# A hybrid decoder layer on one core: the first output gates' weight tile is cast later, and the filling of the attention stage starts from an account of -500

## The chip, the cores and the metric

The kernel runs on one core of one Trainium2 chip, as one launch. The metric is the device time of that core in microseconds. The engines are TensorE (PE in the profile, its weight loads PEld), VectorE (DVE), ScalarE (ACT), GpSimd (POOL) and SyncE (SP), which issues most of the DMAs.

## The reference, cut to what matters

One decoder layer on 1024 tokens and 16 meta tokens, width 1024: half a SwiGLU, a mixer of two parallel head groups, half a SwiGLU again. The change lies in the mixer:

```python
u = rms_norm(h, mix_norm) @ w_in
hq, hf, hi, hg, sq, sk, sv = split(u)
# stick-breaking attention, 8 heads of 64, in blocks of 128 queries
z = q @ k.T * scale
log_beta, log_keep = log_sigmoid(z), log_sigmoid(-z)      # masked to earlier keys
w = exp(log_beta + suffix_sum(log_keep))                  # product of (1 - sigmoid) behind
out = w @ v
# HGRN2, 4 heads: queries, forget gates, values and output gates
f = lb + (1 - lb) * sigmoid(hf);  k = (1 - lb) * sigmoid(-hf)
q = silu(hq);  gate = silu(hg)
```

All of it is float32. The kernel reaches that precision by splitting each operand into a rounded half and the rest, and by three products for each: high by high, low by high, high by low.

## The kernel before, in words

**Stages.** First the first SwiGLU, then the mixer's input projection, the attention (the braid), the HGRN2 heads with the output projection, and the second SwiGLU. TensorE runs in the order in which the program was written there (a manual schedule for that engine alone). The other engines' order is made at compile time by a list scheduler from dependences and the order of writing, and an engine works through its queue in order. `issue_after(x)` sets that what is written inside it stands behind `x`, on `x`'s engine.

**The weights.** `split_w` (L215) loads a 128-column tile of `w_in` into a float32 tile `raw` (L227, a DMA in SyncE's queue, 512 KB; two buffers), lets ScalarE cast it to the high part (L232) and VectorE subtract that for the low part (L234). `col_tile` (L237) is its form for a column.

**The braid** (L1719) runs the attention. A job is a pair of query blocks of one head; the eight heads have four jobs each, with 144 and 272, 912 and 1040, 400 and 528, 656 and 784 keys. In a job there are score pieces (`sb_scores`, L1646): two matmuls into one of two banks `z` (L1665, L1666), two sigmoids on ScalarE (`keep` L1667, `sig` L1668), a running product on VectorE (a scan, L1671, which needs the constant tile `begin`, L2209, in the bank of an earlier projection) and a multiplication on GpSimd (L1678). Two rounds later come its flips: transposes of `sig` into one of two banks (L1515, L1571), split by ScalarE (L1643) and VectorE (L1644). Three rounds later come the products with the values (L1592, L1594). Round n so holds the scores of job n, the flips of job n - 2 and the values of job n - 3.

**The filling.** Between these pieces the braid lays steps of the HGRN2 projections (`hgrn_fill`, L1131), 76 at most. A step is 12 matmuls (L249 to L251), half of a piece of 512 (queries, output gates) or 256 to 272 columns (values, forget gates). The columns go head by head, as values, forget gates, queries, output gates. The first head's values and forget gates are projected ahead of the braid, so the braid's first step belongs to its queries. `part` (L1172) does a step; the first step of each column also takes the next column's tile, so the braid's first step loads and splits the tile of the first output gates. Behind the second half of a piece `use` (L1140) evacuates it: for forget gates two sigmoids on ScalarE (L1154, L1155) into staging tiles `st` (four buffers), two scalings on VectorE (L1156, L1159) and two stores (L1160, L1164); for queries and gates a sigmoid (L1162) and a multiplication (L1163). In the braid the filling has one bank.

**The account.** Every round adds to `owed` 1.22 times the written cost of its own pieces (0.84 for each score column, 107 for each flip, 240 for each value step). While `owed` is above 0 a step is taken and its cost, 12 (0.42 n + 13), is subtracted. The steps of a round are spread evenly over it:

```python
            owed += share * sum(t for _, t, _ in now)
            more = []
            while owed > 0:
                step = next(fill, None)
                if step is None:
                    break
                more.append(step)
                owed -= step[0]
            now += [(at + (i + 0.5) / len(more), t, f) for i, (t, f) in enumerate(more)]
```

Of the kernel before, what the change touches and what calls it, by code (L numbers as in the profile page):

```python
# [15 lines left out]
AF = mybir.ActivationFunctionType  # L16
# [4 lines left out]
P = 128  # L21
# [28 lines left out]
class Block:  # L50
# [161 lines left out]
            (dst[3], lambda r: kept(3, sub, r[0], r[1])),  # L212
        ]

    def split_w(self, view, parts=None):  # L215
        nc = self.nc
        n = int(np.prod(view.shape[1:]))
        if parts is not None:
            got = []
            for i, tag in enumerate(self.w_tags):  # L220
                t = self.wp.tile([P, n], F32R, tag=tag, name="w" + "hl"[i], bufs=self.w_bufs)
                self.last_load = nc.sync.dma_start(t.bitcast(F32), parts[:, i])
                got.append(t)
            return got
        raw = self.wp.tile([P, n], F32, tag="raw", name="raw", bufs=self.raw_bufs)
        to = raw.rearrange("p (k f) -> p k f", k=view.shape[1]) if len(view.shape) == 3 else raw
        self.last_load = nc.sync.dma_start(to, view)  # L227
        hi = self.wp.tile([P, n], F32R, tag="wh", name="wh", bufs=self.w_bufs)
        if self.split_on_vector:
            nc.vector.tensor_copy(hi, raw)  # L230
        else:
            self.rounded = nc.scalar.copy(hi, raw)  # L232
        lo = self.wp.tile([P, n], F32R, tag="wl", name="wl", bufs=self.w_bufs)
        nc.vector.tensor_sub(lo, raw, hi.bitcast(F32))  # L234
        return hi, lo

    def col_tile(self, w, col):  # L237
        return self.split_w(
            w[:, col : col + P].rearrange("(k p) f -> p k f", p=P), self.parted.get(col)
        )  # L240

    def product(self, ps, w, xh, xl, c0, n, ks=None):
# [888 lines left out]
    def hgrn_fill(self, xh, xl, pool, dst):  # L1131

        nc = self.nc
        plan, cols = self.heads_plan, self.columns_of_heads()
        self.stores, self.level_banks = [], "zo"

        def staged(n):
            return pool.tile([P, 512], F32, tag="st", name="st", bufs=4)[:, :n]

        def use(kind, h, ps, c0, n):  # L1140
            s = slice(c0, c0 + n) if kind in "vf" else slice(c0 - META, c0 - META + n)
            t = staged(n)
            if c0 >= HALVES[1][0] and kind != "g":
                ps = ps[:, ::-1]
                at = s.start + HALVES[1][0] + T - 2 * c0 - n
                s = slice(at, at + n)
            if kind == "v":
                nc.scalar.copy(t, ps)
                with self.tc.issue_after(self.last_load.ins):
                    nc.sync.dma_start(dst[kind][h, :, s], t)  # L1150
                return
            elif kind == "f":
                k = staged(n)
                nc.scalar.activation(t, ps, AF.Sigmoid)  # L1154
                nc.scalar.activation(k, ps, AF.Sigmoid, scale=-1.0)  # L1155
                nc.vector.tensor_scalar(  # L1156
                    t, t, self.lbc[:, h : h + 1], self.lb[:, h : h + 1], ALU.mult, ALU.add
                )
                nc.vector.tensor_scalar_mul(k, k, self.lbc[:, h : h + 1])  # L1159
                nc.sync.dma_start(dst["k"][h, :, s], k)  # L1160
            else:
                nc.scalar.activation(t, ps, AF.Sigmoid)  # L1162
                nc.vector.tensor_mul(t, t, ps)  # L1163
            store = lambda: nc.sync.dma_start(dst[kind][h, :, s], t)  # L1164
            if (kind, h) == plan[-1] and c0 == HALVES[1][0]:
                self.stores.append(store)
            else:
                store()

        kept = {}  # L1170

        def part(i, ci, c0, n, half):  # L1172
            if ci == 0 and half == 0:
                kept["w"] = self.ahead_w.pop(cols[i])
                for c in cols[i + 1 : i + (3 if i == 0 else 2)]:
                    if c not in self.ahead_w:
                        self.ahead_w[c] = self.col_tile(self.a["w_in"][0], c)
                kept["round"] = self.rounds[cols[1]]
            if half == 0:
                kept["ps"] = self.proj_bank(n)  # L1180
            self.product(
                kept["ps"], kept["w"], xh, xl, c0, n, range(4 * half, 4 * half + 4)
            )
            if half == 1:
                with self.tc.issue_after(kept["round"]) if i == 0 else ExitStack():
                    use(*plan[i], kept["ps"], c0, n)

        for i, (kind, _) in enumerate(plan):
            for ci, (c0, n) in enumerate(PIECES if kind in "vf" else HALVES):
                for half in range(2):  # L1190
                    yield 12 * (n * 0.42 + 13), lambda a=(i, ci, c0, n, half): part(*a)
# [454 lines left out]
    def sb_scores(self, pool, qs, ks, b, sigs):  # L1646
        nc = self.nc
        nk = META + P * (b + 1)
        pieces = -(-nk // 512)
        size = -(-nk // pieces)  # L1650
        size += size % 2
        q = qs[:, b * P : (b + 1) * P]
        kept = []

        def piece(s0, n):
            last = s0 + n == nk
            if last:
                keep = pool.tile([P, nk + 1], F32, tag="keep", name="keep", bufs=3)
                sig = pool.tile([P, nk], F32, tag="sig", name="sig", bufs=6)
                nc.gpsimd.memset(keep[:, nk : nk + 1], 1.0)  # L1660
                kept.append(keep)
                sigs.append(sig)
            keep, sig = kept[0], sigs[-1]
            z = self.pz.tile([P, n], F32, tag="z", name="z")
            nc.tensor.matmul(z, q, ks[0][:, s0 : s0 + n], start=True, stop=False)  # L1665
            nc.tensor.matmul(z, q, ks[1][:, s0 : s0 + n], start=False, stop=True)  # L1666
            nc.scalar.activation(keep[:, s0 : s0 + n], z, AF.Sigmoid, scale=-1.0)  # L1667
            nc.scalar.activation(sig[:, s0 : s0 + n], z, AF.Sigmoid)  # L1668
            first, end = max(s0, 1), nk + 1 if last else s0 + n
            kv = keep[:, first:end][:, ::-1]  # L1670
            nc.vector.tensor_tensor_scan(  # L1671
                out=kv, data0=kv, data1=self.begin[:, : end - first] if last
                else self.begin[:, :1].broadcast_to([P, end - first]),
                initial=0.0 if last else keep[:, end : end + 1],
                op0=ALU.mult, op1=ALU.max if last else ALU.bypass,
            )
            if s0 == 0:
                nc.gpsimd.tensor_mul(sig, sig, keep[:, 1 : nk + 1])  # L1678

        return [  # L1680
            (n * 0.84, lambda s0=s0, n=n: piece(s0, n))
            for s0 in reversed(range(0, nk, size)) for n in [min(size, nk - s0)]
        ]
# [35 lines left out]
    def braid(self, jobs, fill, share, turn, value):  # L1719


        waiting = []
        owed = 0.0
        at = 0
        while True:
            job = next(jobs, None)
            for lag, steps in zip((0.0, turn, value), job or ()):
                spans = [1.0 if lag == turn else t for t, _ in steps]
                done = 0.0
                for span, (t, f) in zip(spans, steps):  # L1730
                    waiting.append((at + lag + (done + span / 2) / sum(spans), t, f))
                    done += span
            if not waiting:
                break
            now = [x for x in waiting if x[0] < at + 1]
            waiting = [x for x in waiting if x[0] >= at + 1]
# [9 lines that stand above are left out]
            for _, _, f in sorted(now, key=lambda x: x[0]):  # L1746
                f()
            at += 1
# [672 lines left out]
```

## Time and profile before

| | |
|---|---|
| median of 3 runs | 1938.81 us (1938.69 to 1940.38) |
| the profiled execution | 1938.33 us |
| its span, first to last instruction | 1936.6 us |
| TensorE, matmuls busy | 1915.8 us (99%) |
| VectorE busy | 1394.2 us (72%) |
| ScalarE busy | 847.4 us (44%) |
| GpSimd busy | 451.4 us (23%) |
| granted TensorE clock | 1.000 |

Durations in a row are those of one profiled execution. Matmuls are pipelined: a row of 0.39 us can be followed by the next 0.23 us later, and the distance between starts is the price of one. In the rows in order of time the columns are the start in us from the span's start, the length in us, the engine, the line, the operation, what it writes and reads, its shape and how many were merged; brackets give the idle time of that engine before it and what ended it. `proj` is a bank of a projection, `z` one of scores, `flip` one of transposes, `oacc` one of values.

### The profile page before, as it was taken

How to read it: one execution, taken by the hardware profiler on the slowest of the kernel's cores; microseconds unless marked ns; L12 is line 12 of the kernel's file. 1: busy time of each engine (PE TensorE's matmuls, PEld its weight loads, DVE VectorE, ACT ScalarE, POOL GpSimd, SP SyncE). 2: the span in 40 equal slices, each digit the busy share in tenths (PEclk: the TensorE clock that was granted, in tenths of full speed). 3: DMA queues.
4: the chain of work that ended last, by engine and by line, in shares of the span. 5: the costliest groups of instructions: out<-in, count | busy, mean ns of one | idle time of the engine just before them, and what ended most of it. 6: DMA issues, size and time to landing. Idle time of an engine off the chain costs nothing.

```text
span 1936.6 us, 30253 instructions
## 1 busy us (share of the span) xinstructions
PE 1915.8 (99%) x10637; PEld 1620.7 (84%) x10637; DVE 1394.2 (72%) x2184; ACT 847.4 (44%) x1712; POOL 451.4 (23%) x625
## 2 busy tenths in 40 slices
PE   9999999999999999999999999999999999999999
PEld 7888888888888888889998988888888888888887
DVE  7977778877678665567777776667577767766774
ACT  7523343334444545356666635433223332344443
POOL 3010100101000003133333342210545544530000
PEclk9999999999999999999999999999999999999999
DMA  7266788757975416765454178646544444479473
GB/s 220 89 175 169 244 280 257 232 199 272 382 238 183 138 42 154 188 182 150 135 155 123 57 267 246 154 185 211 170 128 133 135 127 134 128 251 315 147 233 114
DMA packets 381687, 355.54 MB, mean 184 GB/s; under 512 B 129040, under 2 KB 284560, under 8 KB 381536
## 3 DMA queue, kind: packets, MB, share of 16 engines
q1 hardware_dynamic: 360768, 288.98, 49.3%
q0 software_dynamic: 20768, 64.63, 9.6%
q8 instruction: 84, 1.38, 0.3%
q14 instruction: 67, 0.55, 0.1%
HBM read 237.95 MB, written 115.57 MB: 183 GB/s over the span
## 4 chain that ended last, share of the span: by engine, by line
PE 92%; DVE 3%; DMA 2%; ACT 1%; issue 1%; SPq 0%; POOL 0%; DVEq 0%; POOLq 0%; ACTq 0%
PE o L735 22%; PE qb L452 18%; PE qc L452 12%; PE qa L452 12%; PE proj L249 5%; PE proj L251 5%; PE proj L250 5%; PE flip L1515 2%; PE wo L250 1%; PE wo L251 1%; PE wo L249 1%; PE mq L1014 1%; PE oacc L1594 1%; PE oacc L1592 1%; PE z L1665 1%
## 5 line engine op out<-in xcount | busy, mean ns | idle before, releaser
L452 PE MATMUL qb<-T,wh 128*128 128x512 f32 x1056 | 343.7, 390 | 1.4 <-DVE u L484 1.4
L452 PEld LDWEIGHTS qb<-T,wh 128*128 128x128 f32 x1056 | 198.2, 188 | 45.8 <-issue 3.5
L452 PE MATMUL qa<-B,wh 128*128 128x512 f32 x696 | 227.6, 392 | 0.3 <-ACT B L838 0.2
L362 DVE TENSOR_TENSOR wl<-s,wh 128x512 fp32r<-128x512 f32 x160 | 165.8, 1036 | 69.1 <-ACT wh L360 68.2
L249 PE MATMUL proj<-xh,wh 128*128 128x512 f32 (+2 forms) x640 | 212.7, 332 | 1.1 <-ACT kT L1391 0.6
L735 PE MATMUL o<-t,w 128*128 128x512 f32 x924 | 212.1, 390 | 0.0
L251 PE MATMUL proj<-xl,wh 128*128 128x512 f32 (+2 forms) x640 | 209.3, 327 | 0.7 <-DVE xl L1984 0.7
L735 PE MATMUL o<-parts 128*128 128x512 f32 x924 | 209.6, 389 | 0.0
L250 PE MATMUL proj<-xh,wl 128*128 128x512 f32 (+2 forms) x640 | 208.9, 326 | 0.0
L452 PE MATMUL qb<-T,wl 128*128 128x512 f32 x528 | 205.6, 389 | 0.0
L735 PEld LDWEIGHTS o<-t,w 128*128 128x128 f32 x924 | 172.8, 188 | 37.1 <-issue 0.8
L735 PEld LDWEIGHTS o<-parts 128*128 128x128 f32 x924 | 173.5, 188 | 36.0
L360 ACT CAST wh<-s 128x512 fp32r<-128x512 f32 x160 | 99.5, 622 | 186.6 <-PE qb L452 141.6
L452 PEld LDWEIGHTS qa<-B,wh 128*128 128x128 f32 x696 | 130.5, 188 | 29.2 <-issue 1.0
L360 ACT CAST wh<-raw 128x512 fp32r<-128x512 f32 x120 | 74.4, 621 | 143.2 <-PE qc L452 101.3
L452 PE MATMUL qa<-B,wl 128*128 128x512 f32 x348 | 135.5, 389 | 0.0
L249 PEld LDWEIGHTS proj<-xh,wh 128*128 128x128 f32 x640 | 120.9, 189 | 12.7 <-ACT st L1155 1.2
L251 PEld LDWEIGHTS proj<-xl,wh 128*128 128x128 f32 x640 | 120.9, 189 | 11.8 <-DVE xl L1984 1.2
L250 PEld LDWEIGHTS proj<-xh,wl 128*128 128x128 f32 x640 | 121.1, 189 | 9.2
L452 PEld LDWEIGHTS qb<-T,wl 128*128 128x128 f32 x528 | 99.1, 188 | 20.3
L452 PE MATMUL qc<-T,wh 128*128 128x512 f32 x352 | 115.9, 391 | 0.0
L452 PE MATMUL qc<-B,wh 128*128 128x512 f32 x352 | 114.6, 389 | 0.0
(400 smaller groups left out, 3832.5 us busy)
## 6 DMA issues: line engine op xcount, KB each, us to landing
raw<-in_ffn_w_in_dram SPq DMA_DIRECT2D x176, 256.0 KB, 3.9
raw<-in_ffn_w_out_dram SPq DMA_DIRECT2D x112, 256.0 KB, 4.5
w2in<-both SPq DMA_DIRECT2D x28, 512.0 KB, 4.0
raw<-in_w_in_dram SPq DMA_DIRECT2D x25, 512.0 KB, 4.3
ks<-kD SPq DMA_DIRECT2D x32, 260.0 KB, 4.8
wout<-both SPq DMA_DIRECT2D x16, 512.0 KB, 3.9
wh<-w2in SPq DMA_DIRECT2D x27, 256.0 KB, 3.1
wl<-w2in SPq DMA_DIRECT2D x27, 256.0 KB, 3.3
```

What stands on the lines that cost most here:

```text
L249: nc.tensor.matmul(ps, wh[:, s], xs, start=k == 0, stop=False)
L250: nc.tensor.matmul(ps, wl[:, s], xs, start=False, stop=False)
L251: nc.tensor.matmul(ps, wh[:, s], xl[:, k, c0 : c0 + n], start=False, stop=k == nk - 1)
L360: nc.scalar.copy(hi, src)
L362: self.block_lo = nc.vector.tensor_sub(lo, src, hi.bitcast(F32))
L452: nc.tensor.matmul(ps, a[:, k, :], b[:, k, :], start=start and k == 0 and i == 0, stop=k == 3 and i == 2, skip_group_check=True,)
L735: nc.tensor.matmul(banks[bank][m], y[:, m * P : (m + 1) * P], z, start=start and at == 0 and e == 0, stop=q == nq - 1 and e == 2, skip_gro ...
L1014: nc.tensor.matmul(ps[at : at + 32, :], self.xm[:, 4 * h + k, :], got[i, h][:, k, :], start=h == 0 and k == 0, stop=h == 1 and k == 3, til ...
L1515: self.nc.tensor.transpose(ps[:m, j, :], src[:, s0 : s0 + m], self.ident)
L1592: nc.tensor.matmul(o[:, c], vj, w[0], start=j == 0, stop=False, skip_group_check=True)
L1594: nc.tensor.matmul(o[:64, c], vj[:, :64], w[1], start=False, stop=end, skip_group_check=True)
L1665: nc.tensor.matmul(z, q, ks[0][:, s0 : s0 + n], start=True, stop=False)
```

## The change

Three things. `split_w` gets a form `late`, which only loads; the rest of it becomes `split_raw`. In the filling's third column (`i == 2`, the first head's queries) the next column's tile, that of the first output gates, is loaded late, and it is split by the following step of the filling, on ScalarE behind the last `sig` written by then. And the braid's account begins at -500.0 instead of 0.0.

```diff
-    def split_w(self, view, parts=None):
+    def split_w(self, view, parts=None, late=False):
...
         self.last_load = nc.sync.dma_start(to, view)
+        return raw if late else self.split_raw(raw)
+
+    def split_raw(self, raw):
+        nc, n = self.nc, raw.shape[1]
         hi = self.wp.tile([P, n], F32R, tag="wh", name="wh", bufs=self.w_bufs)
...
-    def col_tile(self, w, col):
+    def col_tile(self, w, col, late=False):
...
-                        self.ahead_w[c] = self.col_tile(self.a["w_in"][0], c)
+                        self.ahead_w[c] = self.col_tile(self.a["w_in"][0], c, i == 2)
                 kept["round"] = self.rounds[cols[1]]
+            if (i, ci, half) == (2, 0, 1):
+                with self.tc.issue_after(self.last_sig.ins):
+                    self.ahead_w[cols[3]] = self.split_raw(self.ahead_w[cols[3]])
...
-            nc.scalar.activation(sig[:, s0 : s0 + n], z, AF.Sigmoid)
+            self.last_sig = nc.scalar.activation(sig[:, s0 : s0 + n], z, AF.Sigmoid)
...
-        owed = 0.0
+        owed = -500.0
```

Worked through, the two accounts lay these first rounds (z: a score piece with its columns; F: a filling step; t: flips; tm: the meta tokens' flips; v: values):

```
round        before                                  changed
0            z144 F z272                             z144 z272
1            z456 z456 z344 z348 z348                z456 z456 F z344 z348 z348
2            t1 z400 t2 F z264 tm z264               the same
3            t4 z328 v0 F t3 z328 v1 t4 z392         t4 z328 v0 t3 z328 v1 t4 F z392
             t4 F v2 z392 tm                         t4 v2 z392 tm
4            v0 v1 t3 z144 v2 v3 v4 t4 F v5          v0 v1 t3 z144 F v2 v3 v4 t4 v5
             z272 v6 v7 tm v8                        z272 v6 F v7 tm v8
```

From round 5 the count of steps is the same until round 9; it differs again in rounds 9 and 10, 19 and 20, 27 to 30 and 32 to 34.

More of the change, by code (lines that the diff above doesn't have):

```diff
@@ L235, in split_w @@
         return hi, lo
-    def col_tile(self, w, col):
+    def col_tile(self, w, col, late=False):
         return self.split_w(
-            w[:, col : col + P].rearrange("(k p) f -> p k f", p=P), self.parted.get(col)
+            w[:, col : col + P].rearrange("(k p) f -> p k f", p=P), self.parted.get(col), late
         )
```

## Prediction

> **What bounds the kernel now.** I read the page first, then the busy time in stretches around the changed lines, then the chain that ended last, and then each engine's rows in order of time there. The profiled execution took 1938.33 us, of which the span is 1936.6. The page's span, its busy line and its chain:
>
> ```profile
> span 1936.6 us, 30253 instructions
> ...
> PE 1915.8 (99%) x10637; PEld 1620.7 (84%) x10637; DVE 1394.2 (72%) x2184; ACT 847.4 (44%) x1712; POOL 451.4 (23%) x625
> ...
> PE 92%; DVE 3%; DMA 2%; ACT 1%; issue 1%; SPq 0%; POOL 0%; DVEq 0%; POOLq 0%; ACTq 0%
> ```
>
> TensorE carries 92% of the chain, so an edit pays only where TensorE stands still. The change acts in the braid (L1719), from the first scores at 851.09 us to shortly after 1115 us. I worked the planner's arithmetic through for both starting accounts and matched the order for 0.0 to the trace; that gives the times of its rounds. These stretches are rounds 0 to 2 as far as the second filling step, the rest of round 2, then rounds 3, 4, 15, 16, 27 and 33 (length, then busy time of TensorE, weight loads, DVE, ACT, POOL):
>
> ```profile
> 851.09:859.88 8.79, 7.10 (x33) 4.83 (x32) 5.76 (x10) 6.52 (x18) 1.30 (x4) 1.00 0.79 239
> 859.88:863.44 3.56, 3.56 (x21) 3.00 (x20) 3.45 (x7) 1.98 (x7) 2.38 (x3) 1.00 1.06 209
> 863.44:873.43 9.99, 9.66 (x58) 8.04 (x56) 8.67 (x13) 6.98 (x18) 5.31 (x8) 1.00 0.58 169
> 873.43:879.60 6.17, 6.17 (x45) 5.66 (x44) 5.23 (x8) 4.29 (x12) 2.05 (x2) 1.00 0.71 189
> 961.70:969.10 7.40, 6.77 (x46) 6.00 (x45) 5.55 (x10) 5.17 (x14) 2.67 (x4) 1.00 0.41 116
> 969.10:979.20 10.10, 9.14 (x58) 7.91 (x57) 5.32 (x9) 4.87 (x14) 3.58 (x7) 1.00 0.69 179
> 1059.40:1069.40 10.00, 9.80 (x70) 8.89 (x69) 8.65 (x13) 7.79 (x20) 5.77 (x9) 1.00 0.39 126
> 1107.10:1115.40 8.30, 8.30 (x50) 7.17 (x48) 3.42 (x8) 3.37 (x10) 0.73 (x1) 1.00 0.19 65
> ```
>
> TensorE idles 8.79 - 7.10 = 1.69 us at the start, 0.33 in round 3, and almost nothing in rounds 4 and 33. That is the whole prize at the place of the change: about 2 us of 1938. The granted clock is 1.00 throughout. In the chain, this start hangs on one load, that of the tile which the change treats:
>
> ```profile
> 848.42 4.25 DMA raw<-in_w_in_dram
> ```
>
> ACT's rows around it (start, length, idle before in brackets) are those of the forget gates' third and fourth pieces (L1154, L1155), the cast (L232) and the first scores' sigmoids (L1667, L1668):
>
> ```profile
> 850.02 0.39 ACT L1154 ACTIVATE st<-proj 128x256 f32<-128x256 f32 x1 [4.07 <-DMA hg_k<-st]
> ...
> 852.69 1.05 ACT L232 CAST wh<-raw 128x1024 fp32r<-128x1024 f32 x1 [1.97 <-DMA raw<-in_w_in_dram]
> 853.65 0.37 ACT L1154 ACTIVATE st<-proj 128x256 f32<-128x256 f32 x1
> 853.92 0.37 ACT L1155 ACTIVATE st<-proj 128x256 f32<-128x256 f32 x1
> 854.18 0.29 ACT L1667 ACTIVATE keep<-z 128x144 f32<-128x144 f32 x1
> 854.35 0.30 ACT L1668 ACTIVATE sig<-z 128x144 f32<-128x144 f32 x1
> ...
> 854.80 0.42 ACT L1668 ACTIVATE sig<-z 128x272 f32<-128x272 f32 x1
> ...
> 857.71 0.46 ACT L1667 ACTIVATE keep<-z 128x344 f32<-128x344 f32 x1 [0.41 <-POOL sig L1678]
> ...
> 860.83 0.52 ACT L1668 ACTIVATE sig<-z 128x400 f32<-128x400 f32 x1
> 862.93 0.60 ACT L1162 ACTIVATE st<-proj 128x512 f32<-128x512 f32 x1 [1.58 <-PE proj L251]
> ```
>
> ACT stands 1.97 us for the raw tile, and everything behind the cast stands with it. TensorE in the same stretch:
>
> ```profile
> 851.27 0.44 PE L249 MATMUL proj<-xh,wh 128*128 128x512 f32 x1
> ...
> 854.07 0.28 PE L1665 MATMUL z<-ks,qs 128*128 128x272 f32 x1
> ...
> 854.70 0.47 PE L1665 MATMUL z<-ks,qs 128*128 128x456 f32 x1 [0.23 <-ACT sig L1668]
> ...
> 855.28 0.47 PE L1665 MATMUL z<-ks,qs 128*128 128x456 f32 x1
> ...
> 858.57 0.43 PE L1665 MATMUL z<-ks,qs 128*128 128x348 f32 x1 [0.64 <-ACT sig L1668]
> ...
> 859.88 0.48 PE L249 MATMUL proj<-xh,wh 128*128 128x512 f32 x1
> ```
>
> The first filling step runs from 851.27 to 854.07, so it lies just over ACT's wait; the price is paid afterwards, in waits for one of the two score banks.
>
> **The change, part by part.** *The late cast.* The load stays in its step, so SyncE's queue keeps one issue of it; only the cast and the subtraction move, behind the sigmoid of the 400-column score. ACT has a hole there: its row at 862.93 waited 1.58 us, and a cast takes 1.05, so I cost it at nothing on ACT; without the hole it would hold the evacuation at L1162 for 1.05. The tile is first used by the gates' first step, three filling steps after the one whose place now triggers the cast; a step is 2.80 us long by TensorE's rows at 851.27 and 854.07, so there are at least 5.6 us for the cast's 1.05 and the subtraction's 1.23: no wait. The raw buffer is held two steps longer; of the pool's two the next column's load takes the other, so nobody waits for that either. What remains in front of the fourth forget piece is another wait. Its two outputs go into staging tiles that the second piece's stores must leave first:
>
> ```profile
> 848.96 0.61 SPq L1160 DMA_DIRECT2D hg_k<-st  x1
> 849.61 0.43 SPq L1164 DMA_DIRECT2D hg_f<-st  x1
> ```
> ```profile
> hg_k<-st SPq DMA_DIRECT2D x1, 128.0 KB, 4.1
> hg_f<-st SPq DMA_DIRECT2D x1, 128.0 KB, 3.9
> ```
>
> They land at 848.96 + 4.1 = 853.06 and 849.61 + 3.9 = 853.51. So L1154 can start at 853.1 instead of 853.65 and L1155 at 853.55 instead of 853.92: taking the cast away frees half a microsecond of the two, not two.
>
> *The debt.* A filling step costs 12 x (512 x 0.42 + 13) = 2737 in the account. Round 0 pays in 1.22 x 0.84 x (144 + 272) = 426, so with 0 at the start one step lies between the two pieces; with -500 the account stays at -74 and round 0 has none. Round 1 then places it after its two 456-column pieces. What follows: round 3 has one step instead of two, round 4 two instead of one, and single steps move later between rounds 9/10, 19/20, 27 to 30 and 32 to 34. Both plans have placed 74 steps at the end, so nothing moves into the later stage.
>
> *The start, worked out by bounds.* The order that ACT gets is unknown, and decides. If the scores' sigmoids stand ahead of L1154, keep of 144 starts at 851.45; by the rows its sig ends 854.35 + 0.30 - 854.18 = 0.47 later, at 851.92, and the 456 piece follows at 851.97; the sig of 272 ends 855.22 - 854.18 = 1.04 after the keep, at 852.49, so the second 456 comes at 852.55 (pitch 855.28 - 854.70 = 0.58), the filling step at 853.13 and, 2.80 long, the 344 piece at 855.93. Its keep can start about one pair, 0.58, later, at 856.51; from keep of 344 to the third piece's release were 858.57 - 857.71 = 0.86, and from there to the second filling step 859.88 - 858.57 = 1.31: 858.68, which is 1.2 earlier than 859.88. If instead L1154 and L1155 stand first, keep of 144 starts at 853.85, TensorE stands from about 851.45 to 854.37 with no filling step to run, and the same additions give 861.08: 1.2 later. No row decides between them: the row at 850.02 shows this queue put L1154 in front of a store's landing 4.07 us away, the row at 852.69 shows a later-traced instruction ahead of L1154. I take the middle, 0.0, and keep both ends.
>
> *Rounds 3 and 4.* In the new plan round 3, and round 4 up to its first flips, have exactly the order of rounds 15 and 16 in the trace before. Those idle 7.40 - 6.77 = 0.63 (a multiplication on POOL) and 10.10 - 9.14 = 0.96, at this row:
>
> ```profile
> 970.68 0.30 PE L1515 MATMUL flip<-ident,sig 128*128 128x128 f32 x1 [0.95 <-DVE wu L1644]
> ```
>
> The POOL product is early in the new round 3, so I take 0.96 against the 0.33 of now: +0.63, with ends -0.33 and 1.59 - 0.33 = +1.26. DVE will not be ahead enough to remove it:
>
> ```profile
> 853.77 1.23 DVE L234 TENSOR_TENSOR wl<-raw,wh 128x1024 fp32r<-128x1024 f32 x1 [2.65 <-ACT wh L232]
> ...
> 855.69 0.48 DVE L2209 MEMSET begin<- 128x512 f32 x1
> ...
> 856.64 5.14 DVE L1671 TENSOR_TENSOR_SCAN keep<-keep,begin 128x144 f32<-128x144 f32 x6
> ```
>
> The scans need `begin`, which needs L1155 and two scalings; with L1155 at 853.55 `begin` comes about 1.2 earlier, and the 1.23 of the subtraction now lies behind the scans, so DVE reaches round 3 when it does now.
>
> *Round 33* keeps one of two steps: its third flips must wait until the first flips' bank is read by ACT and DVE,
>
> ```profile
> L1643 ACT CAST wu<-flip 128x512 fp32r<-128x512 f32 x48 | 28.6, 597 | 10.7 <-PE flip L1515 10.2
> L1644 DVE TENSOR_TENSOR wu<-flip,wu 128x512 fp32r<-128x512 f32 x48 | 32.5, 678 | 11.2 <-ACT wu L1643 10.9
> ```
>
> 0.60 + 0.68 = 1.28 us, with some 0.6 of other TensorE work between (four matmuls of a value step or two, one flip; an estimate): 0.7 at most, 0 at least (the step is now the cover); I take half, +0.35. The other moved steps exchange orders that the trace has elsewhere, nearly without idle time (round 27 idles 0.20 now): 0.
>
> Sum: 0.0 + 0.63 + 0.35 = +0.98, so 1938.33 + 0.98 = 1939.3. The profiled execution lies 0.48 under the median of the runs, 1938.81, and inside the spread of the shown runs but for 0.36; I leave the forecast at 1939.3.
>
> [...] The longest of the braid's subtractions of this kind lies beside a POOL multiplication:
>
> ```profile
> 1088.06 2.03 POOL L1678 TENSOR_TENSOR sig<-sig,keep 128x1040 f32<-128x1040 f32 x1 [3.34 <-DVE keep L1671]
> ```
> ```profile
> 1088.36 2.81 DVE L234 TENSOR_TENSOR wl<-raw,wh 128x1024 fp32r<-128x1024 f32 x1 [0.29 <-ACT wh L232]
> ```
>
> 2.81 against 1.23 at 853.77, where POOL was idle; the change moves the subtraction to where POOL multiplies the 912 and 1040 columns. [...]
>
> **The rivals.** *First, the gain stands:* the sigmoids go ahead, the start brings -1.2, rounds 3 and 33 cost nothing: 1937.1. If all idle time of the start and of round 3 went, -2.0, and the stores landed early too, about 1936. For it speaks the bracket of 1.97, against it the stores' landing at 853.06.
>
> *Second, slower, by thin rounds:* DVE's work for a round no longer fits under TensorE's where a step was taken out. Round 15, with one step, is the model: with round 16 it idles 1.59. If rounds 3, 27 and 33 each idle as much, against 0.33, 0.20 and 0 now, the price is 4.77 - 0.53 = +4.2: 1942.5. It decides once flips wait over a microsecond in more than one of them. Against it: DVE is busy only 3.42 of 8.30 in round 33.
>
> *Third, the shared access:* the moved subtraction stands behind a POOL multiplication for 2.81 - 1.23 = 1.6, in a round that has no slack on DVE: 1939.3 + 1.6 = 1940.9.
>
> *Fourth, the change does not do what it says:* L1154 stays in front and the stores hold the scores in place of the raw tile: +1.2 at the start, 1940.5; it is the upper end of my start term.
>
> **How the numbers follow.** Forecast 0.56 with its start term between the ends; first rival 0.16; second 0.10; third 0.08; fourth 0.10. A difference of 0.2%, 3.9 us, is about what a measurement of this kernel can tell from no change. Only the second rival and pile-ups of the others reach it upwards (0.13), and downwards only effects in later stages that no row here prices (0.07); within 0.2% is 0.80. The range goes from 1936.0 (first rival with all idle time gone) to 1942.5 (second rival).
>
> **What would show it.** The cast's row behind the sig of 400 without idle time before it; whether L1154 or keep of 144 is first on ACT after 851.3, and TensorE idle of about 0.5 or 2.9 us there; the second filling step at 858.7 or 861.1; flips waiting for DVE in rounds 3 and 4. I am wrong if rounds 0 to 4 together move by more than 2 us, or if the difference arises behind the braid.

## The result and the profile after

| | before | changed |
|---|---|---|
| median | 1938.75 us (1938.13 to 1940.38, 4 runs) | 1947.91 us (1945.36 to 1949.79, 4 runs) |
| ratio of the times | | 1.0046, interval 1.0034 to 1.0058 |
| profiled execution | 1938.33 us, span 1936.6 | 1948.94 us, span 1947.2 |
| granted TensorE clock in the runs | 1.000 in the profiled one | 0.998 to 1.000 |

The change makes the kernel slower by 0.46%, about 8.9 us of 1939 (interval 6.6 to 11.2). The forecast was 1939.3 with a range up to 1942.5, so it was wrong. The lines of the code from L212 on have moved: the cast is L236, the subtraction L238, the forget gates' sigmoids are L1158 and L1159, the scores' matmuls L1672 and L1673, their sigmoids L1674 and L1675, the scans L1678, POOL's multiplication L1685, the flips L1522.

The page's span and busy line of the changed kernel:

```profile
span 1947.2 us, 30241 instructions
...
PE 1918.2 (99%) x10637; PEld 1621.0 (83%) x10637; DVE 1396.1 (72%) x2184; ACT 847.1 (44%) x1712; POOL 451.2 (23%) x625
```

TensorE has the same 10637 matmuls and 2.4 us more busy time (1918.2 - 1915.8); 1.5 of it is one filling step, most of it at a granted clock of 0.50 (4.34 us against 2.80, below). Most of the 10.6 us of span are waits. The first score lies at 851.73 (before: 851.09), so 0.6 came ahead of the braid. The braid, up to the first matmul behind it, takes 275.55 us (before: 266.16), 9.4 more, and what follows it 0.5 more. The extra time is therefore in the braid, where I had looked for about 1 us. ScalarE there, in order of time:

```profile
850.67 0.38 ACT L1158 ACTIVATE st<-proj 128x256 f32<-128x256 f32 x1 [4.07 <-DMA hg_k<-st]
...
853.80 0.38 ACT L1158 ACTIVATE st<-proj 128x256 f32<-128x256 f32 x1 [2.46 <-DMA hg_k<-st]
854.20 0.38 ACT L1159 ACTIVATE st<-proj 128x256 f32<-128x256 f32 x1
854.48 0.29 ACT L1674 ACTIVATE keep<-z 128x144 f32<-128x144 f32 x1
...
855.09 0.43 ACT L1675 ACTIVATE sig<-z 128x272 f32<-128x272 f32 x1
...
864.51 1.07 ACT L236 CAST wh<-raw 128x1024 fp32r<-128x1024 f32 x1
```

The cast did move, to 864.51 and without an idle gap. In its old place ScalarE still stands, 2.46 us, now for the stores that must leave the staging tiles; the sigmoids of the first scores (854.48) come behind that. TensorE meanwhile:

```profile
852.08 0.29 PE L1673 MATMUL z<-ks,qs 128*128 128x272 f32 x1
855.00 0.47 PE L1672 MATMUL z<-ks,qs 128*128 128x456 f32 x1 [2.63 <-ACT sig L1675]
...
856.09 0.50 PE L253 MATMUL proj<-xh,wh 128*128 128x512 f32 x1
856.39 0.63 PE L254 MATMUL proj<-xh,wl 128*128 128x512 f32 x1
856.82 0.63 PE L255 MATMUL proj<-xl,wh 128*128 128x512 f32 x1
...
860.43 0.32 PE L1672 MATMUL z<-ks,qs 128*128 128x344 f32 x1
```

It idles 2.63 us for the sigmoids, since no filling step lies there any more. When the step comes, its matmuls follow each other at 0.43 (856.39 to 856.82), where 0.23 was usual; the step takes 860.43 - 856.09 = 4.34 us against 2.80 before. The busy time in stretches of 1 us shows why (length, busy time of TensorE, weight loads, DVE, ACT, POOL, then granted clock, DMA share, GB/s):

```profile
853.00:854.00 1.00, 0.00 (x0) 0.00 (x0) 0.00 (x0) 0.20 (x1) 0.00 (x0) 1.00 1.09 364
...
855.00:856.00 1.00, 1.00 (x4) 0.70 (x5) 0.78 (x2) 0.81 (x3) 0.00 (x0) 1.00 0.78 228
856.00:857.00 1.00, 1.00 (x5) 0.77 (x4) 0.98 (x3) 1.00 (x3) 0.38 (x1) 0.62 0.69 225
857.00:858.00 1.00, 1.00 (x4) 0.81 (x3) 1.00 (x2) 0.60 (x2) 0.86 (x4) 0.50 0.83 216
858.00:859.00 1.00, 1.00 (x4) 0.71 (x4) 0.89 (x2) 0.00 (x0) 0.05 (x1) 0.50 1.07 271
859.00:860.00 1.00, 1.00 (x5) 0.82 (x4) 0.35 (x1) 0.00 (x0) 0.51 (x1) 0.68 1.02 203
```

Some 1.2 us after TensorE has resumed, the granted clock falls to 0.50, and it stays there for some 3.4 us (0.38/0.5 + 1 + 1 + 0.32/0.5). TensorE counts as 100% busy in these rows, which is why a share of busy time alone does not show the loss.

Now the rounds whose steps moved. The stretches of rounds 3, 4, 5 and 33 (their ends to within half a us) with the same columns, for the changed kernel; then rounds 5 and 33 of the kernel before, which the prediction did not show from end to end:

```profile
866.72:874.51 7.79, 6.82 (x43) 5.67 (x42) 6.53 (x11) 4.80 (x15) 4.54 (x7) 1.00 0.46 139
874.51:884.44 9.93, 9.27 (x56) 7.76 (x56) 8.15 (x11) 5.83 (x14) 3.74 (x6) 1.00 0.66 168
884.44:895.69 11.25, 9.91 (x60) 8.61 (x59) 8.35 (x12) 7.05 (x16) 1.65 (x1) 1.00 0.64 181
...
1115.39:1121.82 6.43, 5.35 (x36) 4.60 (x35) 2.67 (x6) 2.71 (x8) 0.73 (x1) 1.00 0.23 82
```

```profile
879.89:889.84 9.95, 9.95 (x61) 8.88 (x60) 8.26 (x14) 6.68 (x18) 3.42 (x7) 1.00 0.79 196
1107.69:1115.55 7.86, 7.86 (x48) 6.71 (x46) 3.22 (x8) 2.93 (x9) 0.73 (x1) 1.00 0.20 69
```

TensorE's idle time in round 3 is 0.97 (0.33 before), in round 4 0.66, in round 5 1.34 and in round 33 1.08 (all three nearly 0 before). TensorE waits for different things there. In rounds 4 and 33 flips wait for VectorE's copy of the flips before them, with no filling step to cover it. In round 3 VectorE is late, because the moved subtraction lies beside POOL's long multiplication:

```profile
865.65 2.13 DVE L238 TENSOR_TENSOR wl<-raw,wh 128x1024 fp32r<-128x1024 f32 x1
867.71 0.68 DVE L1167 TENSOR_TENSOR st<-st,proj 128x512 f32<-128x512 f32 x1
868.31 0.41 DVE L1651 TENSOR_TENSOR wm<-flip,wm 16x256 fp32r<-16x256 f32 x1
```

```profile
864.68 2.03 POOL L1685 TENSOR_TENSOR sig<-sig,keep 128x1040 f32<-128x1040 f32 x1 [3.22 <-ACT sig L1675]
...
866.86 1.68 POOL L1685 TENSOR_TENSOR sig<-sig,keep 128x400 f32<-128x400 f32 x1
```

The subtraction takes 2.13 us instead of 1.23, and the flips' copy behind it starts only when it and the filling's multiplication are done. In round 5 the scores wait for ScalarE, which has taken the cast of another weight tile ahead of their sigmoids. TensorE's rows behind that are this wait, the flips' wait of round 33 and a last one at the exit of the braid:

```profile
889.55 1.06 ACT L236 CAST wh<-raw 128x1024 fp32r<-128x1024 f32 x1
...
890.98 0.57 ACT L1674 ACTIVATE keep<-z 128x456 f32<-128x456 f32 x1
```

```profile
892.32 0.43 PE L1672 MATMUL z<-ks,qs 128*128 128x348 f32 x1 [1.34 <-ACT sig L1675]
...
1118.00 0.63 PE L1522 MATMUL flip<-ident,sig 128*128 128x128 f32 x4 [1.08 <-DVE wu L1651]
...
1127.28 0.50 PE L253 MATMUL proj<-xh,wh 128*128 128x512 f32 x1 [0.78 <-DVE st L1167]
```

The last row is the first filling step of the next stage. The braid's own last step now lies in round 34, only three value steps ahead of it, and both need the filling's one bank: TensorE waits 0.78 us until VectorE's multiplication has freed it. Before, that step followed without a wait.

Before, no cast stood in that place of round 5: the order of casts on ScalarE is the list scheduler's, and it came out differently when the pieces were written in another order.

To compare all kernels of this study I counted, for every round, what the distances between TensorE's starts exceed an undisturbed row (0.2275 us per 512 columns and 0.0045 per matmul, fitted to rows at full clock). The rounds are told apart by the order in which the program lays its pieces, and round 34 ends with the first matmul behind the braid. Idle time and half clock are both in the count:

| kernel | rounds 0-2 | 3-4 | 5 | 30-34 | others | sum |
|---|---|---|---|---|---|---|
| before | 3.5 | 1.9 | 0.5 | 2.6 | 18.1 | 26.6 |
| changed | 6.1 | 3.9 | 2.1 | 5.5 | 18.3 | 36.0 |
| e1 | 6.5 | 3.1 | 2.1 | 5.5 | 18.4 | 35.6 |
| e2 | 3.0 | 3.3 | 0.5 | 2.6 | 18.1 | 27.5 |
| e3 | 6.1 | 2.3 | 0.5 | 2.6 | 18.1 | 29.6 |
| e4 | 2.7 | 6.3 | 0.5 | 5.5 | 17.9 | 32.9 |
| e5 | 2.5 | 3.9 | 2.1 | 5.5 | 18.4 | 32.4 |
| e6 | 3.5 | 2.0 | 0.5 | 2.6 | 18.1 | 26.7 |
| e7 (without 2.8 of added matmuls) | 2.1 | 3.7 | 0.6 | 5.5 | 18.3 | 30.2 |
| e8 | 3.9 | 3.2 | 0.6 | 5.5 | 18.0 | 31.1 |
| e9 | 2.7 | 6.4 | 0.6 | 2.6 | 18.1 | 30.3 |
| e10 | 2.7 | 3.3 | 0.5 | 5.5 | 18.3 | 30.3 |
| e11 | 3.9 | 2.0 | 0.5 | 2.6 | 18.1 | 27.1 |
| e12 | 2.5 | 2.3 | 0.5 | 2.6 | 18.1 | 26.0 |

So the changed kernel loses 9.4 us more in the braid: 2.6 at the start, 2.0 in rounds 3 and 4, 1.6 in round 5, 2.9 in the last five rounds and 0.2 elsewhere. The other rounds are nearly the same in all fourteen traces, so the losses lie where the order changed, and in round 5. The expectations below quote a rougher count, which left the wait at the exit out of the last rounds (4.56 for 5.5).

### The profile page after: what moved, and what is told of

Its sections match the earlier page's. It is cut to its first block, busy times and chain, and to the rows that moved or that the text cites. A ratio compares the mean times of both kernels' runs of the same rounds, so it can differ in the third digit from the quotient of the medians.

```text
span 1947.2 us, 30241 instructions
## 1 busy us (share of the span) xinstructions
PE 1918.2 (99%) x10637; PEld 1621.0 (83%) x10637; DVE 1396.1 (72%) x2184; ACT 847.1 (44%) x1712; POOL 451.2 (23%) x625
## 3 DMA queue, kind: packets, MB, share of 16 engines
q8 instruction: 84, 1.38, 0.3%
## 4 chain that ended last, share of the span: by engine, by line
PE 73%; issue 18%; DVE 3%; POOL 2%; DMA 2%; ACT 1%; SPq 0%; POOLq 0%; DVEq 0%; ACTq 0%
PE o L739 21%; PE qb L456 10%; PE qa L456 8%; PE qc L456 7%; PE proj L253 5%; PE proj L255 5%; PE proj L254 5%; PE flip L1522 2%; PE wo L255 1%; PE wo L254 1%; PE wo L253 1%; PE oacc L1601 1%; PE oacc L1599 1%; PE z L1672 1%; PE z L1673 1%
```

## The experiments

Two theories stood against each other. The first: the place of the first filling step does it, by the idle stretch and the half clock behind it, and what follows is an echo of that. The second: the rounds that lost a step are too thin for VectorE and ScalarE, wherever they lie, and would cost the same without any trouble at the start. Each experiment's ratio goes with the kernel before on the same chip; its medians there lie between 1938.8 and 1939.2, so differences between medians of two experiments carry some tenths of a us besides their spread.

**e1, the debt without the late cast.** The kernel before with

```diff
-        owed = 0.0
+        owed = -500.0
```

> The account starts at -500, the tile is cast where it was before. Theory A (the first step's place): the time is lost because no filling step lies over ScalarE's wait at the start, so TensorE stands there; the cast in front makes it no better, so +8 to +11 us against before. Theory B (thin rounds: the steps moved later in rounds 3/4, 30 and 33): the same +8 to +11. Theory C (the late split itself: its order on ScalarE and VectorE, and GpSimd's multiplication beside it): only +3 to +5, since the split is undone.

Measured: 1946.26 us (1945.34 to 1947.12) against 1939.17; ratio 1.0039 (1.0026 to 1.0051). Nearly the whole loss is the account's.

**e2, the late cast without the debt.** The changed kernel with `owed = 0.0`.

> The late cast alone, the account at 0. A and B: within 1 us of before, perhaps 0.5 faster, since the filling step still lies over ScalarE's wait. C: +3 to +6.

Measured: 1938.99 us (1936.39 to 1940.0); ratio 1.0000 (0.9991 to 1.0009). The runs show neither gain nor cost from the late cast alone. In its trace 0.4 us less are lost at the start and 1.4 more in rounds 3 and 4, where a filling step waits 1.09 us for VectorE.

**e3, only the first step moved.** The changed kernel, with the account restored behind round 0, so that all other rounds are as before:

```diff
+            if at == 0:
+                owed += 500.0
             at += 1
```

> Late cast, account at -500 for round 0 only and put back by +500 behind it: only the first filling step is moved, all later rounds are as before. A: +5 to +7 (the start, and what VectorE's and ScalarE's later order makes of it). B: +2 at most, 2.6 us of idle time at the start less what the step then covers. The trace should show TensorE idle for over 2.5 us after the second score piece in both.

Measured: 1940.24 us (1938.53 to 1943.95); ratio 1.0007 (0.9998 to 1.0015). The start in its profile is that of the changed kernel, 6.1 us lost and the half clock for 3.4 us. But the time is only some 1.4 us longer, which the interval (-0.4 to 2.9) cannot tell from no change; the trace has 3.0. The first theory alone falls here: the start, with all that follows from it in an otherwise unchanged order, explains about a sixth of the 8.9, a third at most.

**e4, a smaller debt.** The changed kernel with `owed = -400.0`: the first step is back in its place; rounds 3 and 4, 19 and 20 and the last ones keep the new order.

> Late cast, account at -400: by the planner's arithmetic the first step stays between the two first pieces, rounds 9 and 10 too are as before, and rounds 3/4, 19/20, 27 to 34 are those of the changed kernel. A: +2 to +3. B: +6 to +8. The difference to the changed kernel is the price of the first step's place.

Measured: 1943.4 us (1942.95 to 1944.88); ratio 1.0024 (1.0014 to 1.0034). Without the disturbed start there remain some 4.7 us (2.7 to 6.6). The thin rounds cost without it. In its profile the clock is halved in round 3, too, with the first filling step in its old place:

```profile
865.82:869.23 3.41, 3.09 (x11) 2.60 (x11) 3.30 (x6) 1.73 (x5) 1.39 (x3) 0.50 0.80 224
```

**e5, no store in front of the scores.** The changed kernel, with both outputs of a 256-column forget piece in one staging tile of 512, so that the four buffers hold four pieces instead of two:

```diff
-            t = staged(n)
+            both = staged(512) if kind == "f" and n == 256 else None
+            t = staged(n) if both is None else both[:, :n]
...
-                k = staged(n)
+                k = staged(n) if both is None else both[:, n:]
```

> The changed kernel, with both outputs of a 256-column forget-gate piece in one staging tile, so that the fourth piece's sigmoids do not wait for the second piece's stores. Theory A (the start, behind those sigmoids): the 2.6 us of idle time go, and the low clock behind them; 3 to 5 us faster than the changed kernel, +4 to +6 against before. Theory B (thin rounds alone): within 1.5 us of the changed kernel, +8 to +9 against before.

Measured: 1943.51 us (1942.13 to 1945.44) against 1938.97; ratio 1.0024 (1.0015 to 1.0034). ScalarE and TensorE in its profile (lines one further on):

```profile
849.56 0.38 ACT L1159 ACTIVATE st<-proj 128x256 f32<-128x256 f32 x1 [2.17 <-PE proj L255]
...
850.11 0.30 ACT L1675 ACTIVATE keep<-z 128x144 f32<-128x144 f32 x1
```

```profile
850.64 0.47 PE L1673 MATMUL z<-ks,qs 128*128 128x456 f32 x1 [0.64 <-ACT sig L1676]
...
851.74 0.39 PE L253 MATMUL proj<-xh,wh 128*128 128x512 f32 x1
...
854.46 0.32 PE L1673 MATMUL z<-ks,qs 128*128 128x344 f32 x1
```

ScalarE waits for the projection only, TensorE 0.64 instead of 2.63, and the filling step takes 854.46 - 851.74 = 2.72 at full clock. The median is 4.4 us under that of the changed kernel; 4.7 over the kernel before remain, as in e4.

**e6, the same staging in the kernel before.**

> The kernel before, with the same shared staging tile. If ScalarE at the start waited for the stores and not for the raw tile, the start's 1.7 us of idle time shrink: 0.5 to 1.5 us faster than before. If the cast in front decides, ScalarE still stands until the raw tile lands: within 0.5 us of before.

Measured: 1939.38 us (1938.43 to 1941.88); ratio 1.0004 (0.9996 to 1.0013). There the cast stands in front and waits for the raw tile, so that the stores never decided. With e2, where the stores' wait came out as soon as the cast was gone: each of the two waits hides the other.

**e7, the idle stretch filled.** The changed kernel, with twelve matmuls ahead of round 1 whose bank nobody reads:

```diff
+                nc.tensor.matmul(
+                    ps, xh[:, 0, META : META + P], xh[:, 0, META : META + 512], start=True, stop=True
+                )
...
+            if at == 1:
+                self.idle()
```

> The changed kernel with 12 matmuls more, 128x512, whose result nobody reads, in front of round 1's first score piece: they lie in the 2.6 us in which TensorE stands. If the half clock of the filling step behind that wait comes from TensorE's standing, the step takes 2.8 us again instead of 4.3 and the kernel is 1 to 2 us faster than the changed one, although it has 2.8 us more of work. If the clock has another cause: the step stays at 4.3 us and the time within 0.5 us of the changed kernel, or up to 0.5 above.

Measured: 1943.97 us (1943.55 to 1945.38); ratio 1.0029 (1.0017 to 1.004): with work that nobody needs the median is 3.9 us under the changed kernel's. TensorE's rows (lines nine further on):

```profile
851.36 2.91 PE L1179 MATMUL proj<-xh 128*128 128x512 f32 x12
854.51 0.47 PE L1681 MATMUL z<-ks,qs 128*128 128x456 f32 x1 [0.24 <-ACT sig L1684]
...
855.61 0.40 PE L253 MATMUL proj<-xh,wh 128*128 128x512 f32 x1
...
858.37 0.32 PE L1681 MATMUL z<-ks,qs 128*128 128x344 f32 x1
```

The 456-column score comes no earlier, 3.63 us behind the first score (3.27 in the changed kernel), but the filling step behind it takes 858.37 - 855.61 = 2.76 at full clock, not 4.34. So the half clock here comes from TensorE's idleness, not from the scores' lateness. From the first score to the 344 piece it is 1.2 shorter than in the changed kernel. The other cast's place in round 5 changed too, by itself (0.6 lost instead of 2.1); so the 3.9 are not the clock's alone: of the 3.0 by which the braid is shorter in the traces, 1.2 lie at the start and 1.6 in round 5.

**e8, the smaller debt without the late cast.** The kernel before with `owed = -400.0`.

> The account at -400 and the tile cast where it was before: the first step stays in place, the thin rounds 3/4 and 27 to 34 are there, the late split is not. With the late split, this order cost +4.2 us. Theory B (thin rounds by themselves): +3 to +5. Theory C' (the subtraction that the late split puts into round 3 makes that round lose): +1.5 to +2.5, the end of the braid alone.

Measured: 1942.35 us (1940.18 to 1944.48); ratio 1.0019 (1.001 to 1.0028). That is 3.7 us over the kernel before (1.9 to 5.4), as Theory B said, though the interval reaches down to C'. Thin rounds alone so cost, in its trace, 1.2 in rounds 3 and 4 and 2.9 in the last five. Rounds 3 and 4 lose 3.2 here and 6.3 in e4, which differs only in the late cast: on a thin round 3 the cast's subtraction beside POOL's multiplication is a burden. TensorE waits 1.38 us for a flip's copy in e4's round 3 and not in this one, and the half clock that follows it in e4, absent here, is at most 1.7 of the 3.1 (half of 3.41). In the whole time the two lie 1.1 apart, within their intervals.

**e9, only rounds 3 and 4 thin.** The late cast, an account from 0.0, and

```diff
             at += 1
+            owed += {3: -400.0, 4: 400.0}.get(at, 0.0)
```

> The account begins at 0.0, the late cast stays, and only rounds 3 and 4 exchange a filling step (400 taken from the account before round 3 and given back before round 4); every other round is as in the kernel before. Theory that thin rounds cost by themselves: rounds 3 and 4 lost 2.08 us before, 3.64 in the changed kernel and 6.39 with a debt of 400 and the late cast, so the time is 1940.5 to 1943.5. Rival, that the rounds lose only because of what the disturbed start leaves behind: within 0.5 us of the late cast alone, 1938.5 to 1939.5.

Measured: 1941.3 us (1939.42 to 1943.68) against 1938.8; ratio 1.0012 (1.0003 to 1.0021), 2.3 us over the late cast alone by the medians. One exchanged step, with the late subtraction in the thin round, costs this much with an untouched start. VectorE, POOL and TensorE in round 3, then its stretches of 1 us:

```profile
861.63 2.14 DVE L238 TENSOR_TENSOR wl<-raw,wh 128x1024 fp32r<-128x1024 f32 x1
...
864.29 0.41 DVE L1651 TENSOR_TENSOR wm<-flip,wm 16x256 fp32r<-16x256 f32 x1
```

```profile
860.65 2.04 POOL L1685 TENSOR_TENSOR sig<-sig,keep 128x1040 f32<-128x1040 f32 x1 [0.89 <-DVE keep L1678]
```

```profile
864.75 0.55 PE L1522 MATMUL flip<-ident,sig 128*128 128x128 f32 x3 [1.46 <-DVE wm L1651]
```

```profile
863.00:864.00 1.00, 0.29 (x3) 0.04 (x1) 1.00 (x2) 0.78 (x3) 1.00 (x1) 1.00 0.00 0
864.00:865.00 1.00, 0.25 (x2) 0.25 (x3) 1.00 (x3) 0.00 (x0) 0.62 (x2) 1.00 0.00 0
...
867.00:868.00 1.00, 1.00 (x4) 0.81 (x3) 0.89 (x3) 0.39 (x1) 0.92 (x2) 0.50 0.87 226
```

The slow subtraction makes VectorE late, TensorE waits 1.46 for a flip's copy with no filling step to do, and then the clock is halved here too. Here the subtraction begins 0.1 behind round 3's first flips (861.55); in the changed kernel, whose start had set TensorE back, it began 1.1 ahead of them (865.65 against 866.72), and rounds 3 and 4 lost 3.9 instead of 6.4. The clock was halved at the start there and not in these rounds, which is up to 1.7 of the difference. The losses do not simply add up.

**e10, only the last rounds thin.** The late cast, an account from 0.0, and 500 taken from it before round 27.

> The account begins at 0.0 with the late cast, and 500 is taken from it before round 27, so that only rounds 27 to 34 have the changed kernel's order. Theory that the moved steps of the last rounds cost by themselves: rounds 30 to 34 lost 2.56 us before and 4.56 in the changed kernel, so 1940.5 to 1941.5. Rival, that they cost nothing alone (my prediction gave them 0.35): 1939.0 to 1939.5.

Measured: 1941.96 us (1939.67 to 1944.44); ratio 1.0013 (1.0004 to 1.0022). Rounds 30 to 34 lose 5.5, as in the changed kernel and in all others with this order; the largest row is again that of round 33, whose step of cover is gone, and the wait at the exit is again 0.78:

```profile
1111.17 0.63 PE L1522 MATMUL flip<-ident,sig 128*128 128x128 f32 x4 [1.08 <-DVE wu L1651]
...
1120.45 0.50 PE L253 MATMUL proj<-xh,wh 128*128 128x512 f32 x1 [0.78 <-DVE st L1167]
```

**e11, the late cast with shared staging and no debt.** e5 with `owed = 0.0`.

> The account begins at 0.0, the cast is late, and both outputs of a 256-column forget piece share one staging tile, so that neither the raw tile nor the stores stand in front of the scores. Theory that this pair of waits was the whole prize at the start: TensorE's 1.69 us of idle time there shrink by about 1.2, 1937.5 to 1938.3. Rival, that the score banks bind there anyway and nothing moves: 1938.6 to 1939.6.

Measured: 1938.56 us (1936.26 to 1943.8); ratio 1.0003 (0.9993 to 1.0013). With both waits gone from ScalarE nothing is gained that the runs can tell. Its profile shows one reason, in stretches of 1 us:

```profile
855.00:856.00 1.00, 0.64 (x3) 0.30 (x2) 0.79 (x2) 1.00 (x4) 0.00 (x0) 1.00 0.95 245
856.00:857.00 1.00, 0.70 (x3) 0.30 (x2) 1.00 (x1) 1.00 (x3) 0.77 (x2) 1.00 1.20 344
857.00:858.00 1.00, 0.67 (x3) 0.38 (x3) 0.89 (x2) 1.00 (x4) 0.00 (x0) 1.00 0.95 239
858.00:859.00 1.00, 1.00 (x4) 0.81 (x5) 1.00 (x2) 0.65 (x2) 0.55 (x1) 0.52 1.08 228
```

With the filling step still in front of them, round 1's scores run into their two banks, TensorE is busy for 2.01 of 3 us, and the clock drops in this execution. Nine of the eleven runs lie between 1936.3 and 1939.6, the other two, with clocks of 0.998 and 0.999, at 1942.8 and 1943.8. The profiled execution, at 1939.3, is one of the nine, so a drop at this place is not what sets the two apart; what does stays open.

**e12, the first step moved with shared staging.** e5 with the account restored behind round 0, as in e3.

> The changed kernel with shared staging, and with 500 given back to the account after round 0, so that only the first filling step is moved, and with no store in front of the scores. Theory that the step's new place is harmless once the scores wait for nothing: rounds 0 to 2 lost 3.45 us before and 2.39 in the changed kernel with shared staging, so about 1937.9. Rival, that the new place costs by itself: above 1939.5. In either case it should lie 1 to 3 us under the first step alone without shared staging (1940.24).

Measured: 1937.63 us (1935.84 to 1942.81); ratio 0.9995 (0.9986 to 1.0004), 2.6 us under e3 by the medians. The new place of the step is harmless as soon as the scores wait for no store: rounds 0 to 2 lose 2.5 us, as in e5 and less than in all others without added matmuls. It has the lowest median of the study, 1.2 us under the kernel before, which the interval cannot tell from no change.

**The account.** In the traces the 9.4 us are 2.6 at the start, 2.0 in rounds 3 and 4, 1.6 in round 5, 2.9 in the last five rounds (1.1 in round 33, 0.8 at the exit, 1.0 in rounds 30 to 32) and 0.2 elsewhere (0.5 more in round 10, 0.4 less in round 20). In the ratios, of about 1939 us: first step 1.4 (e3), rounds 3 and 4 2.3 (e9), last rounds 2.5 (e10), late cast 0.0 (e2) but contained in all three; together 6.2 of 8.9. Each of these has an interval of about 1.7 to either side. Round 5, which no run isolates, has 1.6 in the trace; this loss is in the three kernels with the whole debt and no added matmul (changed, e1, e5) and in no other, and e7 shows that it goes when the cast gets another place. The 1.1 that are then left are smaller than the intervals. The 0.6 ahead of the braid and the 0.5 behind it lie in the spread of the other kernels there (first score at 849.4 to 851.8, 818.2 to 820.2 us behind the braid).

## Why the prediction was wrong

*The failed step* is the one that priced the moved steps: "+0.63" for rounds 3 and 4, "I take half, +0.35" for round 33, and for all others "exchange orders that the trace has elsewhere, nearly without idle time ...: 0". Measured alone, rounds 3 and 4 cost 2.3 and the last rounds 2.5; in the changed kernel's trace they lost 2.0 and 2.9 more, and round 10, one of the others, 0.5. That "nothing moves into the later stage" was right for the steps, but the step that moved into round 34 left the next stage waiting 0.78 us for its bank. The start term, 0.0 as the middle of two ends, failed as well: 2.6 in the trace, over its upper end of +1.2, though e3's runs leave 1.4 (-0.4 to 2.9). The second rival had the right mechanism and nearly the right sum: it said +4.2 for thin rounds, and the runs with these rounds and the first step in its old place measured 4.7 with the late cast (e4) and 3.7 without it (e8). That the sum came so near is in part luck, as its places were only partly right: rounds 30 to 34 lose, round 27 hardly (0.32 of 8.57 us idle). What I held against it, that DVE is busy for only 3.42 of 8.30 in round 33, was a share over a stretch where the order of one flip, its two copies and the next flip decides; the working of the round 33 term had found the right wait, "0.7 at most", and it measured 1.08.

*Rounds 3 and 4.* Rounds 15 and 16 were the model, 0.96 against 0.33. In the changed kernel idle time there rose by 1.30, from 0.33 to 0.97 + 0.66, just over the upper end of +1.26, and e8, with these rounds thin and no late cast, lost 1.2 more there than the kernel before: the model's upper end was right for the order alone. But the model has no subtraction beside POOL's multiplication, and no half clock. The third rival named that (2.13 here, estimated 2.81) and I kept it apart from the second, where the runs show them as one: by the lost time in rounds 3 and 4 the late subtraction costs 1.4 us where they have their old steps (e2 against before) and 3.1 where they are thin (e4 against e8), the half clock that it brings there included.

*The start.* The order was that of the fourth rival, L1158 first; keep of 144 came at 854.48 (said: 853.85), TensorE idled 2.63 (said: 2.9). The cast found its hole on ScalarE, as said. But the second filling step should then have come at 861.1, and it came at 863.2. Of the 2.1 us between, 0.6 is ScalarE's later start and 1.5 is the half clock (4.34 - 2.80). "The granted clock is 1.00 throughout" was read as a fact of the kernel, when it was a result of TensorE being kept busy: the moved step was itself what kept the clock up there (e3 without it: 0.50 for 3.4 us; e7 with other matmuls in its place: 1.00).

*Round 5*, 1.6 us in the trace, was not in the working at all: that the list scheduler may put a cast elsewhere when the order of writing changes.

*The chances.* The four rivals were treated as alternatives. Three of them came true together (second, third, fourth), and I had left 0.13 to the second and to "pile-ups of the others".

## What to carry to other kernels

The filling steps that covered a wait did three jobs here: they filled the time, they gave the other engines time for their copies (without one, TensorE waited 1.08 us for VectorE's in round 33), and at the start they kept TensorE's clock up (1.00 in the kernel before, 0.50 for 3.4 us in e3, without the step); when a step is moved, price all three at the place it leaves, round by round. If an account or a budget shifts a schedule, do not take the later shifts for zero because each exchanges known orders: run each stretch alone, as here by giving the account its debt and taking it back. Before a wait is taken away, look for the second one beside it (here a store behind a cast): neither shows in the time while the other stands, and the moved step became harmless only with the second one gone too (e12 against e3). Here the two together were worth nothing that the runs can tell (e11). At the end of a stage, ask what the next stage's first instruction needs from the last step.

## What the runs showed of the hardware

TensorE's clock was granted at one half for 3.4 us in the braid of six profiled executions (changed, e1, e3, e4, e9, e11), each time in or behind a stretch of about 3 us in which it was little busy: 2.63 us of idle time on end in the changed kernel, 3.21 in e1 and 3.06 in e3, 1.62 of the last 3 us in e4, 1.20 us of work between 862 and 865 in e9 (0.66 + 0.29 + 0.25), and 2.01 of 3 us in e11. e7 shows that matmuls which nobody needs hold the clock. How busy is busy enough the runs do not show. A stretch of the kernel before, less busy than e11's, kept the full clock in its profiled execution:

```profile
855.87:859.28 3.41, 1.95 (x9) 1.01 (x8) 3.14 (x6) 2.94 (x8) 1.30 (x4) 1.00 0.67 197
```

In the changed kernel, e9 and e11 TensorE was not idle there for more than 2.63 us on end, and in e11 it was two thirds busy. The clock fell at different points of the same wait: 1.2 us after TensorE resumed in the changed kernel (856.24, resumed 855.00), 0.3 after in e1 (854.26, 853.95) and 0.5 ahead of it in e3 (853.20, 853.66). What sets the point, no run here shows.

VectorE's subtraction of 128x1024 took 1.18 to 1.23 us in the changed kernel wherever it did not begin under one of POOL's multiplications. In four rows it did, and each ended 1.07 or 1.08 us behind the multiplication's end, at lengths of 2.13 (865.65), 2.10 (878.73), 1.33 (925.03) and 2.81 (1095.44). POOL's 400-column multiplication, begun under the first of these, took 1.68, where it took 0.90 in the kernel before. The one of 1040 columns, under way when the subtraction began, took 2.03 as against 2.04. What holds up the one that begins later, the rows do not show.
